# Row units moved to other weight steps, constants loaded behind the keys of head 0, and query banks summed into SBUF, in a hybrid attention layer on one Trainium2 core

## The chip, the core and the metric

The kernel runs on one core of a Trainium2 chip. The core has a matrix engine (TensorE, PE in the profile), a vector engine (VectorE, DVE), a scalar engine for activations and copies (ScalarE, ACT), a general engine (GpSimd, POOL) and SyncE (SP), which here only issues transfers. Each engine works through a queue of its own in order. They meet through semaphores. Data lies in SBUF (128 partitions), matmuls write to PSUM (8 banks of 128 x 512 floats), inputs come from HBM by DMA.

The metric is the device time of one execution in microseconds (us). The kernel before took 1256.5 us, the median of 3 runs from 1255.31 to 1256.72.

## What is computed

One layer with 256 latent tokens `x` and 256 context tokens `ctx`, 2048 wide, in float32. The context passes through the same weights and only feeds keys and values.

```python
h   = layer_norm(x)   * (1 + scale)   + shift      # scale, shift from silu(c) @ w_mod
h_c = layer_norm(ctx) * (1 + scale_c) + shift_c
aq, ak, av, az, bq, bk, bv, bz, bg, mga, mgb = split(h @ w_in)     # the same for h_c
y_a = neighbourhood_attention(aq, ak, av, ak_c, av_c, bias)        # 16 heads of 64
y_b = gated_linear_attention(rope(bq), rope(bk), bv, gates(bg), context parts)  # 4 heads
p_a = (y_a * silu(az)) @ w_br_a
p_b = (rms(y_b) * silu(bz)) @ w_br_b
out = (sigmoid(mga) * p_a + sigmoid(mgb) * p_b) @ w_out
x_new = layer_norm(2 ** 0.25 * x + gate * out)
```

## The kernel before

**Precision.** Matmuls run in a rounded float format. Each operand is therefore split into a rounded part and the rest: `split` casts on ACT (`hi`, line 148) and subtracts on DVE (`lo`, line 150). Three matmuls (hi x hi, hi x lo, lo x hi) stand for one product.

**Weights.** `load` (line 155) fetches one unit of weights, 128 x 1024 floats (704 columns for `av`), by SP into a `raw` tile, and splits it into `h_` and `l_` tiles. There are 4 `raw` buffers and 3 each of `hi` and `lo`. The loads are counted; `events` holds work that is hung on a load's number. The matmuls of a unit follow. The loads of the part that matters here: 1 to 4 are the queries `aq` of attention pairs 0 and 1, 5 to 12 the values `av` of group 0; 13 to 24 and 25 to 36 are the same for pairs 2, 3 and 4, 5; 37 and 38 are `aq6`, 39 and 40 the keys `ak7`, 41 and 42 `aq7`; 43 to 46 are the keys of head 0 of the gated linear attention (`keys(0)`), 47 to 50 its queries, 51 to 58 keys and queries of head 1, and so on.

**Row units.** `attended` needs the normalised tokens with tokens in rows, split, in chunks of 128 columns. `rows_of_h` (line 410) makes them, in 8 units of two chunks. A unit has three steps. `fetch_and_scale` issues two DMAs on SP behind the DMA of its load, `xr` (the tokens) and `sb` (the modulation, from a scratch tensor in HBM); both go to `raw` tiles; then eight DVE instructions (lines 425 and 426) scale and shift. `parts` splits the result into `rh` and `rl`, which release the `xr` tile. `store` writes both to `hrows` in HBM by two DMAs on SP. Before, unit n fetches at load 6 + 6n, splits at 7 + 6n and stores at 11 + 6n, so the last one at loads 48, 49 and 53. `rh` and `rl` come from `staging` (line 407), two buffers in all, which the constants `cs` (rope tables) and `wg` (gate weights) use as well.

**Constants.** Lines 635 to 644, behind the set-up of the last attention pair and ahead of `keys(0)`: four DMAs on POOL's queue (`cs`, `wr`, `bgt`, `ngt`) and the split of `wr` into `wg`. `gates` reads `wg` for the last time in head 3, `rope_of` reads `cs` for the last time there too.

**Query banks.** `project_x` (line 374) multiplies the latent tokens with a unit pair. It leaves two halves of a PSUM bank, 256 columns each, whose sum is the result. ACT copies the upper half to SBUF (`low`), DVE adds it to the lower half in the bank. The callers read the bank then: `project_pair` (line 475) makes `qh` and `ql` with four ACT and four DVE instructions on 64 partitions each (lines 493 to 500), `queries` (line 693) scales it on ACT, and `gated_a` (line 848) takes a sigmoid and a product of it. The banks of the pairs, `acc`, are four; `value_columns` (line 576) needs all four for its tiles `va`.

**Order.** The program is written in one order, and a planner orders each engine's queue from it ahead of time: an instruction that comes earlier in the program goes first among those that its model thinks ready. `issue_after` pins some behind others. A tile of a tag with few buffers takes one that the planner thinks free. [...]

**Head 0 to `attended`.** After the attention pairs come `keys(0)`, `turn_gates`, `gates(0)`, `queries(0)` and `decayed(0)`, and then heads 1 and 2. `attended(0)` (line 793) takes heads 0 and 1 through 16 passes: `gather` fetches a chunk of `hrows` to a `raw` tile (`hr`) and multiplies it with the weights of attention (12 matmuls, `g`), `project` loads a unit of `wv` and multiplies (12 matmuls, `o`). Between passes 7 and 9 it starts head 2's scores, `gates(3)`, and keys, queries and `decayed(3)` of head 3. `attended(1)` does heads 2 and 3.

Of the kernel before, what the change touches and what calls it, by code (L numbers as in the profile page):

```python
# [8 lines left out]
F32 = mybir.dt.float32  # L9
F32R = mybir.dt.float32r  # L10
U8 = mybir.dt.uint8
AF = mybir.ActivationFunctionType
ALU = mybir.AluOpType
# [3 lines left out]
P = 128  # L17
D = 2048
KT = 16
T = 256  # L20
# [4 lines left out]
NH = 4  # L25
# [3 lines left out]
NEG = -1.0e30  # L29
NC = 4  # L30
HELD = 4
SHARES = (
    ((0, 512, False), (512, 512, True), (1024, 512, False), (1536, 512, False)),
    ((0, 512, False), (512, 256, True), (1024, 512, False), (768, 256, True), (1536, 256, False), (1792, 256, False)),
# [54 lines left out]
def tile_backbone_layer(  # L89
# [21 lines left out]
    nc = tc.nc  # L111
    const = ctx.enter_context(tc.tile_pool(name="const", bufs=1))
# [12 lines left out]
    def k4(shape, name, dt=F32):  # L125
        return work.tile(shape, dt, tag="k4", name=name, bufs=4)

    def k2(shape, name, dt=F32):
        return work.tile(shape, dt, tag="k2", name=name, bufs=5)
# [13 lines left out]
    def mm(o, a, b, start, stop):  # L143
        return nc.tensor.matmul(o, a, b, start=start, stop=stop).ins  # L144
# [8 lines left out]
    loads, events = [], {}  # L153
# [12 lines left out]
    def unit(name, k):  # L166
        return load(wst[UNIT_AT[name, k]], 1024, f"{name}_{k}")
# [203 lines left out]
                mm(dst, wl[:, c], hhi[:, 0:2, a, :], False, False)  # L371
                mm(dst, wh[:, c], hlo[:, 0:2, a, :], False, a == KT - 1)

    def project_x(name, dst):
        for k in range(0, KT, 8):
            wh, wl = unit(name, k)
            for i in range(8):
                a = k + i
                c = slice(P * i, P * i + P)
                if a:  # L380
                    mm(dst[:, :T], wl[:, c], hhi[:, 0, a, :], False, False)
                mm(dst, wh[:, c], hl[:, :, 0, a, :], a == 0, a == KT - 1)
                if a == 0:
                    mm(dst[:, :T], wl[:, c], hhi[:, 0, a, :], False, False)
        low = k2([P, T], f"low_{name}")
        nc.scalar.copy(low[:], dst[:, T:])
        nc.vector.tensor_tensor(out=dst[:, :T], in0=dst[:, :T], in1=low[:], op=ALU.add)

    def project_rows(dst, wh, wl, k, w, tiles):
        for t in range(tiles):  # L390
# [16 lines left out]
    def staging(shape, name, dt=F32R):  # L407
        return const.tile(shape, dt, tag="staging", name=name, bufs=2)
# [31 lines left out]
        return fetch_and_scale, parts, store  # L440

    for n in range(8):
        events.setdefault(6 + 6 * n, []).append(lambda dma, sub, n=n: rows_event(n, dma, sub))

    def rows_event(n, dma, sub):
        fetch, parts, store = rows_of_h(n)
        fetch(dma, sub)
        events.setdefault(7 + 6 * n, []).insert(0, parts)
        events.setdefault(11 + 6 * n, []).insert(0, store)

    store_modulation()

# [12 lines left out]
    for p in range(K0):  # L465
        dst = kTs[p // 4][:, p % 4, :]
# [8 lines left out]
    def project_pair(p, q):  # L475
        kT = kTs[p // 4][:, p % 4, :]
        if p >= K0:
            kp = acc(f"kp{p}")
            project_t(f"ak{p}", kp[:])
            nc.scalar.copy(kT, kp[:])  # L480
        kn = k2([P, 512], f"kn{p}", F32R)
        kl = k2([P, 512], f"kl{p}", F32R)
        split(kn[:], kl[:], kT, loads[-2] if p >= 2 else None)
        kh = k4([P, 2, 512], f"kh{p}", F32R)
        for j in range(2):
            for r, src in zip(half, (kn, kl)):
                nc.gpsimd.dma_start(kh[r, j, :], src[half[j], :])
        qp = acc(f"qp{p}")
        project_x(f"aq{p}", qp[:])
        qh, ql = q[:, p % 2, 0], q[:, p % 2, 1]  # L490
        for j in range(2):
            r, o = half[j], half[1 - j]
            nc.scalar.mul(qh[r, j, :], qp[r, :T], 0.125)
            nc.vector.scalar_tensor_tensor(
                ql[r, j, :], qp[r, :T], 0.125, qh[r, j, :].bitcast(F32), ALU.mult, ALU.subtract
            )
            nc.scalar.mul(qh[o, j, :], qp[r, :T], 0.125)
            nc.vector.scalar_tensor_tensor(  # L498
                ql[o, j, :], qp[r, :T], 0.125, qh[r, j, :].bitcast(F32), ALU.mult, ALU.subtract
            )  # L500
        return qh, ql, kh

    def attention(p, qh, ql, kh):
# [70 lines left out]
    low = []  # L574
# [19 lines left out]
    def turn_gates():  # L594
        lp = bank("lp")
        for t in range(4):
            nc.tensor.transpose(lp[:, P * t : P * t + P], low[0][:, t].rearrange("p r c -> p (r c)"), ident[:])
        nc.scalar.copy(lr[:], lp[:])
        for r in (slice(32, 64), slice(96, 128)):
            nc.vector.tensor_tensor(out=lr[r, :], in0=lp[r, :], in1=lr[r, :].bitcast(F32), op=ALU.subtract)  # L600

    probs = {}
    for g in range(3):
# [4 lines left out]
        n = len(loads) + 1  # L608
# [13 lines left out]
    n = len(loads)  # L622
# [9 lines left out]
    at(n + 14, (read_values, 7))  # L632


    cs = staging([P, 3, T], "cs", F32)
    wg = staging([P, 2, 512], "wg")
    wr = k4([P, 2, 512], "wr")
    bgt = const.tile([P, NH, 2], F32, name="bgt")
    ngt = const.tile([P, 4], F32, name="ngt")
    for t, src in ((cs, rope), (wr, wg2), (bgt, bg2), (ngt, ng)):  # L640
        nc.gpsimd.dma_start(t[:], src)
    nc.scalar.copy(wg[:], wr[:])
    lo = slice(64, 128)
    nc.vector.tensor_tensor(out=wg[lo], in0=wr[lo], in1=wg[lo].bitcast(F32), op=ALU.subtract)
    def rope_of(dst, src, name, eng):
        t = k2([P, 2, T], f"rt_{name}")
        for a in range(2):
# [6 lines left out]
    def gates(h):  # L654
        zp = pair(f"z{h}")
        for d in range(2):
            mm(zp[:, d, :], wg[:, d, P * h : P * h + P], lr[:], True, True)
        ga = k4([P, 2, 512], f"ga{h}")
        gm = k4([P, 2, 512], f"gm{h}")
        for d in range(2):  # L660
            b = bgt[:, h, d : d + 1]
            nc.scalar.activation(ga[:, d, :], zp[:, d, :], AF.Abs, bias=b)
            nc.vector.tensor_scalar(gm[:, d, :], zp[:, d, :], b, 0.0, ALU.add, ALU.min)
        nc.scalar.activation(ga[:], ga[:], AF.Exp, scale=-1.0)
        nc.scalar.activation(ga[:], ga[:], AF.Ln, bias=1.0)
        nc.vector.tensor_tensor(out=gm[:], in0=gm[:], in1=ga[:], op=ALU.subtract)

        cum = k2([P, 2, T], f"cum{h}")
        dec = k2([P, 2, T], f"dec{h}")

        def scan(o, i):
            nc.vector.tensor_tensor_scan(o, i, i, 0.0, ALU.add, ALU.bypass)

        scan(cum[:, 0, :], gm[:, 0, :T])
        scan(cum[:, 1, :][:, ::-1], gm[:, 1, :T][:, ::-1])
        nc.vector.memset(dec[:, 0, T - 1 : T], 0.0)
        nc.vector.memset(dec[:, 1, 0:1], 0.0)
        scan(dec[:, 0, : T - 1][:, ::-1], gm[:, 0, T + 1 :][:, ::-1])
        scan(dec[:, 1, 1:], gm[:, 1, T : 2 * T - 1])
        nc.scalar.activation(dec[:], dec[:], AF.Exp, scale=1.0 / 16.0)  # L680
        return cum, dec

    def keys(h, own=None):
        kf = k4([P, 2, 512], f"kf{h}")
        for a in range(2):
            bp = acc(f"bk{h}{a}")[:] if own is None else own[:, a, :]
            project_t(f"bk{h}{a}", bp)
            nc.scalar.copy(kf[:, a, :], bp)  # L688
            if hooks:
                hooks.pop(0)()  # L690
        return kf

    def queries(h, room=acc):
        qf = k2([P, 2, T], f"qf{h}")
        for a in range(2):
            bp = room(f"bq{h}{a}")
            project_x(f"bq{h}{a}", bp[:])
            nc.scalar.mul(qf[:, a, :], bp[:, :T], 1.0 / 16.0)
        return qf

    def decayed(h, cum, dec, kf, qf):
# [145 lines left out]

    def gated_a(p, room=acc):
        zp = room(f"az{p}")
        project_x(f"az{p}", zp[:])  # L850
        sg = k2([P, T], f"sga{p}")
        nc.scalar.activation(sg[:], zp[:, :T], AF.Sigmoid)
        nc.vector.tensor_tensor(out=sg[:], in0=sg[:], in1=zp[:, :T], op=ALU.mult)
        nc.vector.tensor_tensor(out=ya[:, p, :], in0=sg[:], in1=ya[:, p, :], op=ALU.mult)

    pws = [weights_of(0)]
    kf = keys(0)
    turn_gates()
    decays = gates(0)
    kq = kf, queries(0)  # L860
    parts = decayed(0, *decays, *kq)
    decays = gates(1)
    kq = keys(1), queries(1)
    parts1 = decayed(1, *decays, *kq)
    hooks.append(lambda: scores(0, parts, pws[0]))
    kf = keys(2)
    decays = gates(2)
    kq = kf, queries(2)
# [151 lines left out]
    fin, gb, zs, zt0 = tail[:, 0:4], tail[:, 4], (tail[:, 5], tail[:, 6]), tail[:, 7]  # L1020
# [3 lines left out]
    for g in range(4):  # L1024
        bp = bank(f"gb{g}")
# [53 lines left out]
    for u in range(8):  # L1079
        src = wst[UNIT_AT[f"wo{NC - 1}", 2 * u]]  # L1080
        if u < HELD:
            raw = stream.tile([P, 1024], F32, tag="raw", name=f"r_last{u}", bufs=4)
# [3 lines left out]
            split(wh, wl, raw[:])  # L1086
        elif u == HELD:
            raw = stream.tile([P, 1024], F32, tag="raw", name=f"r_last{u}", bufs=4)
# [38 lines left out]
    op = acc("wol_0")  # L1127
    last_mm(op[:], 0, 0, 512)
    residual(op[:], 0, NC - 1, base, base + 512, nc.vector)
    finish(0, *statistics(0, NC), SHARES[0])  # L1130
    for i in range(2):
        op = acc(f"wol_1{i}")
# [9 lines left out]
    r, q = tiny([P, 1], "rr"), tiny([P, 1], "rt")  # L1142
# [109 lines left out]
```

## Time and profile before

| what | value |
|---|---|
| median of 3 runs | 1256.5 us |
| the profiled execution's own time | 1255.54 us |
| its span, from the first to the last instruction | 1253.8 us |
| granted TensorE clock, mean | 0.99 |
| read from HBM, written to it | 247.66 MB, 10.52 MB |
| hardware DMA queue of SP (q1) | 59.3% of 16 engines' span |

The profile comes from one execution. A page shows each engine's busy time as a share of the span, and groups of instructions by line. `out<-in` names the tile that is written and those that are read; `xN` is the number of instructions. In the list of waits, `A <- B` says that engine A's instruction stood idle until B was done. A busy matrix engine means that a matmul was in flight. Matmuls overlap, so the distance of their starts is shorter than one takes by itself.

### The profile page before, as it was taken

Reading aid. Unit: us, or ns where it says so; the run is one execution under the profiler, and the core shown is the slowest. Engines: PE = TensorE matmul, PEld = TensorE weight load, DVE = VectorE, ACT = ScalarE, POOL = GpSimd, SP = SyncE. Lnnn points to the kernel's source line nnn. Section 1 sums busy time; section 2 is a strip of 40 time slices with the busy share of each in tenths; the row PEclk is TensorE's granted clock in tenths of the full one; section 3 lists DMA queues with packets and bytes.
Section 4 is the critical chain, followed back from the end, with each engine's and each line's share of the span. In section 5 each row is a group of like instructions: output and inputs, shape, how many; then the busy total and the mean of one; then the engine's idle time right before and its main releaser. Section 6 shows DMA issues by size and latency. Waiting matters only on the chain.

```text
span 1253.8 us, 16294 instructions
## 1 busy us (share of the span) xinstructions
PE 1211.8 (97%) x6233; PEld 996.4 (79%) x6233; DVE 773.4 (62%) x1154; ACT 545.2 (43%) x776; POOL 64.2 (5%) x87
## 2 busy tenths in 40 slices
PE   6999999999999999899899999999999999999997
PEld 5666798989878887678688888888888888888885
DVE  6655577667667565434553366676566665665677
ACT  4322455545455353533353274454444444445350
POOL 1000100000101210001000000000000000000111
PEclk9999999999999999999899999999999999999999
DMA  9997557666623333443745557777776777756661
GB/s 378 418 405 278 149 171 217 198 185 229 190 94 118 118 135 101 155 165 101 252 158 194 190 199 264 237 224 242 240 242 231 246 236 235 237 186 257 243 220 67
DMA packets 77054, 263.45 MB, mean 210 GB/s; under 512 B 8920, under 2 KB 8936, under 8 KB 71856
## 3 DMA queue, kind: packets, MB, share of 16 engines
q1 hardware_dynamic: 73616, 256.69, 59.3%
q0 software_dynamic: 2928, 5.16, 1.8%
q8 instruction: 49, 0.80, 0.3%
q10 hardware_dynamic: 432, 0.56, 0.1%
q14 instruction: 29, 0.24, 0.1%
HBM read 247.66 MB, written 10.52 MB: 206 GB/s over the span
## 4 chain that ended last, share of the span: by engine, by line
PE 79%; DVE 8%; DMA 7%; ACT 3%; issue 2%; POOL 0%; SPq 0%; DVEq 0%; ACTq 0%; POOLq 0%
PE bz L144 7%; PE mgb L144 7%; PE va L144 7%; PE pb L144 7%; PE mga L144 7%; PE kp L144 7%; PE bk L144 7%; PE g L144 5%; PE o L144 5%; PE pa L144 3%; PE wo L144 3%; DMA r_wv<-in_wst 3%; PE az L144 3%; PE bq L144 2%; PE qp L144 2%; PE gp L144 2%
## 5 line engine op out<-in xcount | busy, mean ns | idle before, releaser
L144 PE MATMUL va<-h_av,hl 128*128 128x352 f32 x384 | 97.7, 330 | 6.1 <-DVE q L498 6.1
L144 PE MATMUL kp<-hl,h_ak 128*128 128x512 f32 x256 | 87.1, 408 | 2.2 <-ACT hl L305 2.2
L144 PE MATMUL g<-ah,hr 128*128 128x512 f32 x256 | 82.4, 403 | 3.9 <-DMA hr<-hrows 3.2
L144 PE MATMUL o<-h_wv,gt 128*128 128x512 f32 x256 | 85.1, 395 | 0.2 <-ACT h_wv L148 0.2
L144 PE MATMUL bk<-hl,h_bk 128*128 128x512 f32 x256 | 80.8, 392 | 0.7 <-ACT kf L688 0.7
L144 PE MATMUL bz<-h_bz,hl 128*128 128x512 f32 x256 | 80.6, 392 | 0.0
L150 DVE TENSOR_TENSOR l_wv<-r_wv,h_wv 128x1024 fp32r<-128x1024 f32 x32 | 39.1, 1224 | 67.0 <-ACT h_wv L148 66.9
L144 PE MATMUL mgb<-h_mgb,hl 128*128 128x512 f32 x256 | 79.7, 390 | 0.0
L144 PE MATMUL mga<-h_mga,hl 128*128 128x512 f32 x256 | 79.4, 389 | 0.0
L144 PE MATMUL pb<-h_pb,hl 128*128 128x512 f32 x256 | 79.4, 389 | 0.0
L144 PEld LDWEIGHTS va<-h_av,hl 128*128 128x128 f32 x384 | 68.4, 191 | 8.0 <-DVE q L498 4.3
L150 DVE TENSOR_TENSOR l_pb<-r_pb,h_pb 128x1024 fp32r<-128x1024 f32 x32 | 39.2, 1225 | 39.9 <-ACT h_pb L148 39.9
L144 PEld LDWEIGHTS kp<-hl,h_ak 128*128 128x128 f32 x256 | 48.1, 190 | 19.3 <-issue 5.3
L144 PE MATMUL va<-l_av,hl 128*128 128x352 f32 x192 | 62.5, 325 | 0.0
L144 PEld LDWEIGHTS g<-ah,hr 128*128 128x128 f32 x256 | 48.9, 193 | 16.2 <-DMA hr<-hrows 5.2
L148 ACT CAST h_wv<-r_wv 128x1024 fp32r<-128x1024 f32 x32 | 33.5, 1049 | 56.0 <-DMA r_wv<-in_wst 56.0
L150 DVE TENSOR_TENSOR l_mgb<-r_mgb,h_mgb 128x1024 fp32r<-128x1024 f32 x32 | 39.2, 1225 | 30.1 <-ACT h_mgb L148 29.9
L144 PEld LDWEIGHTS bk<-hl,h_bk 128*128 128x128 f32 x256 | 48.1, 188 | 11.3 <-ACT kf L688 1.1
L144 PEld LDWEIGHTS o<-h_wv,gt 128*128 128x128 f32 x256 | 48.1, 189 | 11.0 <-ACT h_wv L148 1.4
L150 DVE TENSOR_TENSOR l_mga<-r_mga,h_mga 128x1024 fp32r<-128x1024 f32 x32 | 39.2, 1224 | 27.5 <-ACT h_mga L148 27.5
L144 PEld LDWEIGHTS mga<-h_mga,hl 128*128 128x128 f32 x256 | 48.1, 188 | 9.9
L144 PEld LDWEIGHTS pb<-h_pb,hl 128*128 128x128 f32 x256 | 48.1, 188 | 9.9
(335 smaller groups left out, 2975.4 us busy)
## 6 DMA issues: line engine op xcount, KB each, us to landing
wm<-in_wmod SPq DMA_DIRECT2D x32, 1024.0 KB, 9.1
hr<-hrows SPq DMA_DIRECT2D x32, 512.0 KB, 3.7
r_wv<-in_wst SPq DMA_DIRECT2D x32, 512.0 KB, 3.6
r_bz<-in_wst SPq DMA_DIRECT2D x32, 512.0 KB, 3.6
wg<-in_wgate SPq DMA_DIRECT2D x64, 256.0 KB, 3.7
r_mga<-in_wst SPq DMA_DIRECT2D x32, 512.0 KB, 3.6
r_mgb<-in_wst SPq DMA_DIRECT2D x32, 512.0 KB, 3.4
r_pb<-in_wst SPq DMA_DIRECT2D x32, 512.0 KB, 3.3
```

The costliest lines, as they stand in the source:

```text
L144: return nc.tensor.matmul(o, a, b, start=start, stop=stop).ins
L148: cast = nc.scalar.copy(hi, src)
L150: sub = nc.vector.tensor_tensor(out=lo, in0=src, in1=hi.bitcast(F32), op=ALU.subtract)
```

## The change

It has four parts. First, the row units hang on loads 6, 11, 17, 22, 28, 32, 36 and 41, split one load later and store four loads later (before: five loads after the fetch), so the last store hangs on load 45, the third load of `keys(0)`. Second, the constants are fetched and split behind `keys(0)`. Third, `queries(0)` stands ahead of `gates(0)`. Fourth, `project_x` no longer writes back to the bank: ACT copies the upper half, scaled, into an SBUF tile `both`, DVE adds the scaled lower half to it there, and the callers read `both`. `queries` does the same into its own `qf` tile.

```diff
+ROW_STEPS = (6, 11, 17, 22, 28, 32, 36, 41)
...
-    def project_x(name, dst):
+    def project_parts(name, dst):
...
-        low = k2([P, T], f"low_{name}")
-        nc.scalar.copy(low[:], dst[:, T:])
-        nc.vector.tensor_tensor(out=dst[:, :T], in0=dst[:, :T], in1=low[:], op=ALU.add)
+
+    def project_x(name, dst, scale=1.0):
+        project_parts(name, dst)
+        both = k2([P, T], f"both_{name}")
+        nc.scalar.mul(both[:], dst[:, T:], scale)
+        nc.vector.scalar_tensor_tensor(both[:], dst[:, :T], scale, both[:], ALU.mult, ALU.add)
+        return both
...
-        events.setdefault(6 + 6 * n, []).append(lambda dma, sub, n=n: rows_event(n, dma, sub))
+        events.setdefault(ROW_STEPS[n], []).append(lambda dma, sub, n=n: rows_event(n, dma, sub))
...
-        events.setdefault(7 + 6 * n, []).insert(0, parts)
-        events.setdefault(11 + 6 * n, []).insert(0, store)
+        events.setdefault(ROW_STEPS[n] + 1, []).insert(0, parts)
+        events.setdefault(ROW_STEPS[n] + 4, []).insert(0, store)
...
-        project_x(f"aq{p}", qp[:])
+        qs = project_x(f"aq{p}", qp[:], 0.125)
         qh, ql = q[:, p % 2, 0], q[:, p % 2, 1]
         for j in range(2):
             r, o = half[j], half[1 - j]
-            nc.scalar.mul(qh[r, j, :], qp[r, :T], 0.125)
-            nc.vector.scalar_tensor_tensor(
-                ql[r, j, :], qp[r, :T], 0.125, qh[r, j, :].bitcast(F32), ALU.mult, ALU.subtract
-            )
-            nc.scalar.mul(qh[o, j, :], qp[r, :T], 0.125)
-            nc.vector.scalar_tensor_tensor(
-                ql[o, j, :], qp[r, :T], 0.125, qh[r, j, :].bitcast(F32), ALU.mult, ALU.subtract
-            )
+            for d in (r, o):
+                nc.scalar.copy(qh[d, j, :], qs[r, :])
+                nc.vector.tensor_tensor(
+                    out=ql[d, j, :], in0=qs[r, :], in1=qh[r, j, :].bitcast(F32), op=ALU.subtract
+                )
...
-            project_x(f"bq{h}{a}", bp[:])
-            nc.scalar.mul(qf[:, a, :], bp[:, :T], 1.0 / 16.0)
+            project_parts(f"bq{h}{a}", bp[:])
+            nc.scalar.mul(qf[:, a, :], bp[:, T:], 1.0 / 16.0)
+            nc.vector.scalar_tensor_tensor(qf[:, a, :], bp[:, :T], 1.0 / 16.0, qf[:, a, :], ALU.mult, ALU.add)
...
-        project_x(f"az{p}", zp[:])
+        zs = project_x(f"az{p}", zp[:])
         sg = k2([P, T], f"sga{p}")
-        nc.scalar.activation(sg[:], zp[:, :T], AF.Sigmoid)
-        nc.vector.tensor_tensor(out=sg[:], in0=sg[:], in1=zp[:, :T], op=ALU.mult)
+        nc.scalar.activation(sg[:], zs[:], AF.Sigmoid)
+        nc.vector.tensor_tensor(out=sg[:], in0=sg[:], in1=zs[:], op=ALU.mult)
...
     pws = [weights_of(0)]
     kf = keys(0)
+    cs = staging([P, 3, T], "cs", F32)
+    wg = staging([P, 2, 512], "wg")
+    wr = k4([P, 2, 512], "wr")
+    bgt = const.tile([P, NH, 2], F32, name="bgt")
+    ngt = const.tile([P, 4], F32, name="ngt")
+    for t, src in ((cs, rope), (wr, wg2), (bgt, bg2), (ngt, ng)):
+        nc.gpsimd.dma_start(t[:], src)
+    nc.scalar.copy(wg[:], wr[:])
+    lo = slice(64, 128)
+    nc.vector.tensor_tensor(out=wg[lo], in0=wr[lo], in1=wg[lo].bitcast(F32), op=ALU.subtract)
     turn_gates()
+    qf = queries(0)
     decays = gates(0)
-    kq = kf, queries(0)
+    kq = kf, qf
     parts = decayed(0, *decays, *kq)
```

The ten lines of the constants are removed from lines 635 to 644, unchanged.

More of the change, by code (lines that the diff above doesn't have):

```diff
@@ L632, in tile_backbone_layer @@
     at(n + 14, (read_values, 7))
[L635 to L644, printed above, removed]
     def rope_of(dst, src, name, eng):
```

## The prediction

> **What bounds the kernel now.** I read the page first: its first part says that TensorE (PE) is busy nearly all the time.
>
> ```profile
> span 1253.8 us, 16294 instructions
> PE 1211.8 (97%) x6233; PEld 996.4 (79%) x6233; DVE 773.4 (62%) x1154; ACT 545.2 (43%) x776; POOL 64.2 (5%) x87
> ```
>
> PE is idle for 1253.8 - 1211.8 = 42 us in all, so no edit of this kind can give more than that and what a slow clock costs. The view by stretches says where the idle time lies (columns: stretch, its length, busy time of each engine with its instructions, granted clock, DMA share, GB/s).
>
> ```profile
> 141.00:335.00 194.00, 187.94 (x1140) 171.13 (x1139) 135.32 (x225) 98.99 (x186) 16.60 (x33) 0.98 0.65 200
> 335.00:404.00 69.00, 65.96 (x329) 52.75 (x329) 50.48 (x96) 36.15 (x60) 7.01 (x5) 1.00 0.35 118
> 482.00:602.00 120.00, 109.13 (x483) 86.38 (x481) 52.99 (x86) 43.34 (x59) 4.16 (x6) 0.98 0.44 148
> 602.00:735.00 133.00, 132.41 (x600) 109.97 (x600) 54.39 (x75) 52.30 (x78) 2.87 (x3) 0.98 0.58 195
> ```
>
> 141 to 335 holds the pairs of attention heads and the values, 335 to 404 head 0 of the gated linear attention, 482 to 602 the first half of `attended(0)` with the keys of head 3 pushed into it, 602 to 735 its end and `attended(1)`. PE lacks 6, 3 and 11 us in the first three and 0.6 in the last. The waits of PE, over 141 to 480 and then over 480 to 760, name what ended them (total us, times, longest).
>
> ```profile
> PE va L144 <- DVE q L498: 6.1, 3, 2.5
> PE az L144 <- DVE l_az L150: 2.5, 1, 2.5
> PE bq L144 <- DVE l_bq L150: 1.2, 1, 1.2
> PE z L144 <- ACT pr L526: 0.8, 1, 0.8
> PE bq L144 <- ACT h_bq L148: 0.6, 1, 0.6
> PE z L144 <- DVE lr L600: 0.3, 1, 0.3
> ...
> PE ap L144 <- DVE near L743: 3.6, 1, 3.6
> PE g L144 <- DMA hr<-hrows: 3.2, 4, 1.2
> PE o L144 <- DVE l_wv L150: 1.5, 1, 1.5
> PE ap L144 <- DVE near L744: 0.8, 1, 0.8
> ...
> PE bk L144 <- DVE l_bk L150: 0.6, 1, 0.6
> ```
>
> An idle gap costs more than itself here. Behind four of these waits the same view by stretches shows half a clock:
>
> ```profile
> 156.80:160.20 3.40, 3.19 (x10) 2.94 (x11) 3.31 (x10) 1.80 (x4) 0.00 (x0) 0.51 0.00 0
> 214.80:218.20 3.40, 3.40 (x11) 3.11 (x12) 1.24 (x2) 0.78 (x1) 0.00 (x0) 0.50 0.88 279
> 518.60:522.00 3.40, 3.40 (x10) 2.64 (x9) 1.20 (x4) 1.37 (x2) 0.00 (x0) 0.50 0.43 154
> 600.50:607.30 6.80, 6.04 (x17) 4.60 (x17) 2.48 (x9) 0.00 (x0) 0.52 (x1) 0.50 0.90 314
> ```
>
> 3.4 us at half clock lose 1.7 us, the last row 3.4. The first two follow waits for `q`, the third the wait for `l_wv`, the last the wait for `near`.
>
> **Query banks: project_x into SBUF.** Now the two halves of a bank are added inside PSUM, and then four ACT and four DVE instructions read that bank one after the other; a bank is shared by no two engines at once. The bank goes to a `va` tile of the values only when the last of them is done. The chain around the first wait, from the timeline of DVE and PE:
>
> ```profile
> 155.92 0.48 DVE L425 SCALAR_TENSOR_TENSOR xr<-xr,mvs,sb 128x256 f32<-128x256 f32 x1 [3.03 <-DMA sb<-mods]
> 156.44 0.43 DVE L498 SCALAR_TENSOR_TENSOR q<-qp,q 64x256 fp32r<-64x256 f32 x1
> 157.01 0.63 PE L144 MATMUL va<-h_av,hl 128*128 128x352 f32 x1 [2.47 <-DVE q L498]
> ...
> 217.98 7.78 PE va L144 x48
> ```
>
> DVE sat 3.03 us in its queue for the rows' `sb`, the last `q` of the first pair stood behind it, and PE behind that. (The last row is from the chain that ended last: 48 matmuls in 7.78 us, 0.16 each.) After the change a bank is free after two instructions: one ACT copy and one DVE add. The work does not shrink: five instructions stay five on each engine. The new copies and subtractions out of SBUF are not in the trace in their form. The nearest rows bound them:
>
> ```profile
> L497 ACT ACTIVATE q<-qp x16: 375/379/382, 150.7 to 340.2; 64x256 fp32r<-64x256 f32 x16
> L148 ACT CAST kn<-kT 128x512 fp32r<-128x512 f32 x7 | 4.3, 619 | 0.0
> L648 DVE TENSOR_TENSOR qr<-qf,cs x8: 409/422/426, 383.0 to 592.5; 128x256 f32<-128x256 f32 x8
> ```
>
> An ACT copy takes 0.38 (nearest in size, taken) to 0.62, so at most 4 x 0.24 = 1 us more ACT per pair, and a DVE subtraction about 0.42, which is what it takes now. ACT has 95 us free in 141 to 335, so neither is on the path; without that cover the 8 pairs would cost up to 8 us. `both` holds one of five `k2` buffers some 3 us longer than `low` did (eight instructions of 0.38 to 0.43), and the next pair's `kn` and `kl` need two: I take 0 for it. The queries of the heads lose one ACT instruction per bank, also beside the path; `gated_a` keeps its count.
>
> What the path gains: the second and third waits (6.1 - 2.5 = 3.6 us) go, since two instructions of 0.4 us free a bank where ten did; with them one half-clock stretch, 1.7. At the first wait the row unit keeps its step (6), so DVE again waits for `sb`, and the add for the *second* pair can stand behind it and end near 156.9. PE then only gets on by the six matmuls of the tile that has the first bank: 6 x 0.16 = 1.0, and the gap shrinks to 1.5, at the edge of the slow clock; I leave the stretch in. **Term 1: 3.6 + 1.7 + 1.0 = 6.3 us**, between 1 (only the first effect) and 6.1 + 3.4 = 9.5.
>
> **Row units by load 45, constants behind keys(0).** Eight row units go through two `staging` tiles, and so do `cs` and `wg`. The tile views show that the units did not run when their steps say:
>
> ```profile
> L148 ACT CAST rh<-xr x8: 1044/1049/1051, 161.6 to 594.9; 128x1024 fp32r<-128x1024 f32 x8
> L150 DVE TENSOR_TENSOR rl<-xr,rh x8: 1217/1226/1226, 164.8 to 598.2; 128x1024 fp32r<-128x1024 f32 x8
> L435 SPq DMA_DIRECT2D hrows<-rl x8: 360/462/473, 170.5 to 599.5; - x8
> L419 SPq DMA_DIRECT2D xr<-in_xrow x8: 328/345/346, 146.5 to 348.5; - x8
> ```
>
> The last `xr` was fetched at 348.5 and split only at 594.9, just after the last reader of `cs` had begun (592.5, in the `qr` row above). The `parts` of units 6 and 7 come at loads 43 and 49, behind the constants in program order, so those held both staging tiles until head 3 was through, and two fetched `xr` kept two of the four `raw` buffers from about 350 to 595. In the new order the `parts` of unit 7 come at load 42, ahead of the constants, and all buffers are free by about 350. What that cost is seen in `attended(0)` against `attended(1)`, in the chain that ended last:
>
> ```profile
> 530.62 1.24 DVE l_wv L150
> 531.88 4.01 DMA r_wv<-in_wst
> 537.00 1.24 DVE l_wv L150
> ...
> 728.84 5.44 PE o L144 x24
> ```
>
> With two buffers `l_wv` frees the buffer, the next `r_wv` is fetched into it and is split: 537.00 - 530.62 = 6.4 us a pass. A pass is 24 such matmuls, 5.44 us by the last row, and with four buffers PE does it without a gap (602 to 735 above). So the waits on `hr` (3.2), `l_wv` (1.5, with 1.7 of half clock) and `l_bk` (0.6) go: 7.0. The wait for `near` (3.6 + 0.8 + 3.4 of half clock = 7.8) has two of the late units' `rl` (1.23 each) in its DVE queue, and it stands there only because the rows for the last four passes were not stored yet; with them stored, PE has passes to do meanwhile. I count 6 of the 7.8, since the order is the planner's. **Term 2: 13 us**, between 7 and 14.8.
>
> The queues: a unit issues four DMAs on SP as before, only closer (loads 28, 32, 36, 41), and four DMAs for the constants go behind the `kh` copies on POOL, which has 5% work. `wg`'s cast now stands in ACT's queue behind unit 7's store, with the splits of `bq` behind it. The bounds are 0 and the 7.4 that `cs` waits for such a store on POOL now:
>
> ```profile
> POOL cs L641 <- DMA hrows<-rl: 7.4, 1, 7.4
> ```
>
> I take 0.5, since the store leaves with load 45 and PE then has two loads of keys, 5.44 us each, and the queries ahead of `gates(0)`.
>
> **gates(0) behind queries(0).** The four waits of `z` and `bq` (0.3 + 0.8 + 1.2 + 0.6 = 2.9) go with row unit 7 and the gate chain out of that stretch. But the chain's DVE work moves to where `decayed(0)` already fills it:
>
> ```profile
> 370.00:404.00 34.00, 31.80 (x156) 25.42 (x157) 28.82 (x63) 18.60 (x32) 7.01 (x5) 1.00 0.38 130
> L672 DVE TENSOR_TENSOR_SCAN cum<-gm 128x256 f32<-128x256 f32 x8 | 5.1, 677 | 0.1
> ```
>
> Four scans of 0.68, the subtraction L666 over 1024 columns like `rl` (1.23) and two `gm` additions over 512 (an estimate: 0.7 each) make 5.4. 28.8 + 5.4 = 34.2 of 34 us: full, and it spills. The bounds are 0 (the four loads of `keys(1)` alone, 24 matmuls each, give PE 4 x 5.44 = 22 us before it needs `decayed(0)`) and 5.4 + 1.7 x 2 = 8.8, if the splits of `bk` are late and two slow stretches follow. I take 2.4. **Term 3: 2.9 - 2.4 - 0.5 = 0.** The `az` wait (2.5) comes from head 2's rope chain, which the change leaves as it is: 0.
>
> **Sum.** 6.3 + 13 + 0 = 19.3; 1253.8 - 19.3 = 1234.5 us of span. The profiled execution took 1255.5 for its 1253.8, so 1236.2; it stood 1.0 under the median of 1256.5: **1237**.
>
> **Rivals.** *DVE fills up behind queries(0)*: the spill costs its bound, 8.8 instead of 2.4, and Term 1 stays at 3. For it: the 34.2 of 34; against it: three loads can be split ahead. 1237 + 6.4 + 3.3 = 1247. Chance 0.11.
>
> *The planner again gives the constants the staging tiles early*, so the change doesn't do what it says: Term 2 is lost, 1250. Against it: in this trace the units behind the constants in program order got their tiles last. 0.04.
>
> *Slower: DVE's queue waits for sb*, as in the 155.92 row. All eight units wait, and the new steps put more of them next to the banks' adds and the splits:
>
> ```profile
> DVE xr L425 <- DMA sb<-mods: 9.6, 4, 3.8
> ```
>
> Where PE is not covered, such a wait costs up to 3.8 + 1.7 = 5.5. Four of eight eat the gain; with five the time is 1237 + 27 = 1264. Against it: of the four waits now only one stops PE at once. 0.08.
>
> *The slow clock does not come from these gaps*: then the stretches that I took off (1.7 + 1.7 + 2.6 of 3.4) stay, 1243. The trace is against it: each stands right behind a wait. 0.05. The Trainium skill, "TensorE: Matmul & The Clock Gate", section "The HAM clock gate", gives half rate after at least one idle window of about 3.4 us. By that rule only the wait of 3.6 could slow the clock; the trace does not agree, since waits of 1.5 and 2.5 us did too.
>
> *More than forecast*: every wait quoted goes, `az` too with 1.7 for its clock: 9.5 + 14.8 + 2.9 + 4.2 = 31.4, 1225. 0.10.
>
> **How the numbers follow.** The forecast itself (1229 to 1244) has 0.62. From 1225 to 1250 lie the forecast, the clock rival, and most of the first rival and of the better case: 0.8. A measurement can tell about 0.2% (2.5 us) from no change. Faster 0.87; same 0.05, from the upper ends of the first two rivals; slower 0.08.
>
> **What would show it.** Right: no wait of `va` on `q` over 1.6 us; the last `rh` before 350; passes of 5.4 us in `attended(0)`; no slow stretch around 519 and 600. Wrong: `rh` after 500 still; a wait of `bk` or `bq` on `l_bk`, `l_bq` between 360 and 420 beyond 2.4 us in all; new waits of `va` on `l_av` behind idle DVE time ended by `sb`.

## The result and the profile after

| | before | after |
|---|---|---|
| median of the runs side by side | 1256.4 us (1255.3 to 1256.7, 4 runs) | 1223.7 us (1221.6 to 1226.5, 4 runs) |
| profiled execution | 1255.5 us | 1226.5 us |
| its span and granted clock | 1253.8 us, 0.990 | 1224.8 us, 0.998 |

The ratio of the times is 0.974, 95% interval 0.972 to 0.976: 32.7 us less by the medians, 29.0 by the two profiled executions. The profiled execution of the changed kernel is the slowest of its four. The forecast of 1237 was 13 us too high, and the range (1225 to 1250) missed the time by 1.3 us. The time is that of the rival called "more than forecast" (1225), though most of its terms are not.

The page of the changed kernel, its first part:

```profile
span 1224.8 us, 16303 instructions
PE 1200.0 (98%) x6233; PEld 991.0 (81%) x6233; DVE 772.7 (63%) x1154; ACT 542.6 (44%) x768; POOL 64.0 (5%) x87
```

PE is idle for 24.8 us where it was 42. So 17 of the 29 us are idle time; the other 12 are in PE's *busy* time, 1211.8 before and 1200.0 now, for the same 6233 matmuls. The waits of PE in the changed kernel, over 141 to 480 and, last row, over 480 to 760 (total us, times, longest):

```profile
PE s L145 <- DVE q L500: 0.9, 2, 0.8
PE va L145 <- DVE both_aq L391: 0.9, 1, 0.9
PE az L145 <- DVE l_az L151: 0.7, 1, 0.7
PE s L145 <- ACT q L499: 0.6, 1, 0.6
PE o L145 <- ACT gt L149: 0.5, 1, 0.5
...
PE bk L145 <- ACT kf L680: 0.7, 1, 0.7
```

The waits for `q` before `va`, for `near`, `hr`, `l_wv`, `l_bk`, `pr` and `l_bq` are gone, `az` is down from 2.5 to 0.7, and new are the waits of the scores `s` for `q` (1.5 us in 3) and shorter ones of `o` for `gt`. The tile view of the row units shows that they now run when their steps say:

```profile
L149 ACT CAST rh<-xr x8: 1028/1048/1050, 160.9 to 315.7; 128x1024 fp32r<-128x1024 f32 x8
L151 DVE TENSOR_TENSOR rl<-xr,rh x8: 1212/1224/1226, 163.3 to 317.9; 128x1024 fp32r<-128x1024 f32 x8
```

The last `rh` starts at 315.7, not at 594.9, and in `attended(0)` the chain that ended last is PE alone. Each pass is 2.72 + 2.72 = 5.44 us, with nothing between:

```profile
488.37 2.72 PE o L145 x12
491.09 2.72 PE g L145 x12
493.81 2.72 PE o L145 x12
```

**Stretches of the same work.** To set kernels side by side I cut each one where PE starts the same matmul: number 954 (the first of `qp`), 2090 (the first of `bk`), 2820 (the first `g` of `attended(0)`) and 3990 (the first `bz`). Between two of these every kernel here runs the same number of matmuls, so a longer stretch is a cost, as far as its length repeats. The view by stretches, cut at those places, before (columns as in the prediction):

```profile
141.20:334.50 193.30, 187.24 (x1137) 170.51 (x1136) 134.86 (x224) 98.29 (x184) 16.40 (x32) 0.98 0.65 199
334.50:481.80 147.30, 141.80 (x734) 118.31 (x733) 102.49 (x208) 73.81 (x120) 20.05 (x18) 0.99 0.34 114
481.80:751.10 269.30, 257.84 (x1172) 210.45 (x1171) 120.07 (x180) 109.33 (x157) 7.03 (x8) 0.98 0.51 173
```

And after:

```profile
141.20:330.40 189.20, 186.60 (x1138) 168.82 (x1136) 139.12 (x234) 100.30 (x186) 15.86 (x31) 0.99 0.71 219
330.40:470.60 140.20, 139.38 (x734) 117.02 (x732) 98.94 (x194) 71.05 (x112) 17.52 (x18) 1.00 0.36 122
470.60:720.90 250.30, 248.91 (x1172) 208.01 (x1171) 118.75 (x185) 107.43 (x154) 9.98 (x9) 1.00 0.51 174
```

I call them A (pairs and values; Term 1), B (heads 0 to 2 up to `attended(0)`; Term 3 and the `az` wait) and C (`attended(0)` and `attended(1)` with head 3; Term 2). A lost 4.1 us, B 7.1, C 19.0; the rest of the kernel is 643.9 before and 645.1 after.

### The profile page after: what moved, and what is told of

Read it like the earlier page. It is cut to its first block, busy times and chain, and to the rows that moved or that the text cites. A ratio compares the mean times of both kernels' runs of the same rounds, so it can differ in the third digit from the quotient of the medians.

```text
span 1224.8 us, 16303 instructions
## 1 busy us (share of the span) xinstructions
PE 1200.0 (98%) x6233; PEld 991.0 (81%) x6233; DVE 772.7 (63%) x1154; ACT 542.6 (44%) x768; POOL 64.0 (5%) x87
## 4 chain that ended last, share of the span: by engine, by line
PE 78%; DVE 8%; DMA 8%; ACT 3%; issue 2%; POOL 0%; SPq 0%; DVEq 0%; ACTq 0%; POOLq 0%
PE bz L145 7%; PE mgb L145 7%; PE pb L145 7%; PE mga L145 7%; PE o L145 7%; PE g L145 7%; PE kp L145 6%; PE bk L145 5%; PE pa L145 4%; PE bq L145 3%; PE wo L145 3%; PE az L145 3%; PE va L145 2%; DMA sb<-mods 2%; PE gp L145 2%
## 5 line engine op out<-in xcount | busy, mean ns | idle before, releaser
L151 DVE TENSOR_TENSOR l_wv<-r_wv,h_wv 128x1024 fp32r<-128x1024 f32 x32 | 39.2, 1225 | 72.9 <-ACT h_wv L149 72.8
L145 PE MATMUL g<-ah,hr 128*128 128x512 f32 x256 | 79.0, 390 | 0.0
L151 DVE TENSOR_TENSOR l_pb<-r_pb,h_pb 128x1024 fp32r<-128x1024 f32 x32 | 39.2, 1225 | 39.9 <-ACT h_pb L149 39.9
L151 DVE TENSOR_TENSOR l_mgb<-r_mgb,h_mgb 128x1024 fp32r<-128x1024 f32 x32 | 39.2, 1225 | 30.1 <-ACT h_mgb L149 29.9
L145 PEld LDWEIGHTS bz<-h_bz,hl 128*128 128x128 f32 x256 | 48.1, 188 | 9.9
```

Of the source, the lines that this page charges most:

```text
L151: sub = nc.vector.tensor_tensor(out=lo, in0=src, in1=hi.bitcast(F32), op=ALU.subtract)
```

## The experiments

Times in us. "Before" was run again beside each group of kernels: its median was 1255.6 for the first four, 1254.1 for the next four, 1255.7 for the last three. A, B and C are from each profiled execution, cut as above.

| kernel | A | B | C | median (range) | ratio to before, 95% |
|---|---|---|---|---|---|
| before | 193.3 | 147.3 | 269.3 | 1256.4 | 1 |
| after | 189.2 | 140.2 | 250.3 | 1223.7 (1221.6 to 1226.5) | 0.972 to 0.976 |
| banks only | 184.7 | 147.3 | 268.7 | 1246.7 (1246.1 to 1246.9) | 0.991 to 0.996 |
| new steps only | 193.8 | 141.8 | 251.8 | 1235.3 (1233.0 to 1237.8) | 0.981 to 0.987 |
| after, old banks | 195.2 | 140.2 | 252.6 | 1233.7 (1231.9 to 1237.4) | 0.979 to 0.987 |
| after, two buffers held | 186.5 | 140.9 | 262.7 | 1236.9 (1235.6 to 1237.3) | 0.983 to 0.988 |
| after, gates(0) first | 191.1 | 142.4 | 250.4 | 1226.4 (1224.6 to 1230.6) | 0.975 to 0.980 |
| after, old steps | 184.0 | 141.0 | 251.8 | 1223.5 (1222.5 to 1224.7) | 0.972 to 0.977 |
| after, later scores | 185.1 | 140.2 | 250.9 | 1222.5 (1221.5 to 1226.7) | 0.972 to 0.977 |
| ... and later first units | 184.7 | 140.2 | 250.7 | 1222.2 (1220.6 to 1224.7) | 0.972 to 0.976 |
| after, one buffer held | 185.1 | 140.2 | 250.5 | 1223.0 (1222.5 to 1224.4) | 0.972 to 0.976 |
| constants moved only | 191.8 | 141.9 | 253.1 | 1235.1 (1232.5 to 1238.5) | 0.981 to 0.986 |
| after, a second profile | 186.3 | 140.2 | 250.9 | 1223.4 (1221.8 to 1224.1) | 0.972 to 0.976 |

The theory after the result: three parts add up, the banks (A), the row units in time (C, through the `raw` buffers and the stored rows), and what late units did to B. The rivals: one part does all; or a part gains only together with another; or the buffers have nothing to do with it.

### The banks alone

The kernel before with the sums of the query banks taken into SBUF (`project_x`, `project_parts`, and their uses for pairs, queries and gates), and nothing else:

```diff
-        project_x(f"aq{p}", qp[:])
+        qs = project_x(f"aq{p}", qp[:], 0.125)
...
-            nc.scalar.mul(qh[r, j, :], qp[r, :T], 0.125)
...
+                nc.scalar.copy(qh[d, j, :], qs[r, :])
```

> The kernel before with the query banks summed into SBUF alone; row units, constants and gates as before. Theory (the terms add up): the waits of va on q (6.1 us and two slow stretches of 1.7) fall to about 1 us, the late row units stay: 1256.4 - 8 = 1248, between 1245 and 1251; the last rh still near 595. Rival (the wait for sb in DVE's queue is what stops PE, and the bank only shows it): va waits on both instead of q for 4 us or more, 1253 or above.

Measured: 1246.7, 8.9 less than before. All of it is in A; B and C stand as before:

```profile
140.80:325.50 184.70, 183.83 (x1137) 167.92 (x1137) 134.19 (x224) 98.58 (x184) 16.47 (x33) 1.00 0.69 209
325.50:472.80 147.30, 142.09 (x734) 118.06 (x733) 103.25 (x205) 70.93 (x113) 17.94 (x17) 0.99 0.34 114
472.80:741.50 268.70, 257.74 (x1172) 210.54 (x1171) 121.25 (x184) 109.80 (x156) 9.97 (x9) 0.98 0.51 173
```

The clock of A is 1.00 where it was 0.98: both slow stretches behind waits for `q` went, and the first wait, for which I had left 1.5 us and its slow stretch in, is 0.9 and slows nothing. B has its old length from other parts: `az` waits 1.3 us with no slow stretch behind it, and a slow one at 366.0, behind waits of `bq` and `z`, is new.

### The new steps alone

The kernel before with the row units' steps changed; the constants stay ahead of keys(0):

```diff
+ROW_STEPS = (6, 11, 17, 22, 28, 32, 36, 41)
...
-        events.setdefault(6 + 6 * n, []).append(lambda dma, sub, n=n: rows_event(n, dma, sub))
+        events.setdefault(ROW_STEPS[n], []).append(lambda dma, sub, n=n: rows_event(n, dma, sub))
```

> The kernel before with the new row steps alone; constants stay ahead of keys(0), banks as before. Theory: staging tiles go out in the program order of their first writers, so unit 7's parts at load 42 come ahead of the constants and this alone frees the raw buffers: rh ends before 350, passes of 5.4 us in attended(0), 1256.4 - 17 = 1239, between 1235 and 1243. Rival (the constants must stand behind keys(0), or the planner gives them the tiles early): rh after 500 as before, 1252 or above.

Measured: 1235.3, 20.3 less. It is in B (5.5) and C (17.5), and A is no shorter (193.8 to 193.3). My Term 2 had 13 for this edit together with the constants' place.

### The whole change without the banks

The changed kernel with `project_x` and its uses as before:

```diff
-        qs = project_x(f"aq{p}", qp[:], 0.125)
+        project_x(f"aq{p}", qp[:])
...
-        zs = project_x(f"az{p}", zp[:])
+        project_x(f"az{p}", zp[:])
```

> The changed kernel with the query banks added in PSUM again, as before. Theory: the waits of va on q come back, 1223.7 + 8 = 1232, between 1229 and 1236. Rival (new steps alone took the units away from the banks, so the banks' edit is worth little): 1224 to 1227.

Measured: 1233.7, 10.0 over the changed kernel, and 6.0 of the profiled 8.4 are in A (195.2 to 189.2); 2.3 are in C, where `g` waits 1.9 us for `sga`, the tile that `gated_a` makes of its bank. The parts add up: 8.9 (banks) + 20.3 (steps) = 29.2 of 32.7, and the rest is the order of gates(0) (1.6 in B: 141.8 to 140.2 between these two kernels) and scatter of a few us.

### Two raw buffers held

The changed kernel, in which two of the four `raw` buffers belong to idle tiles from keys(0) to the end of decayed(3) (328.7 to 586.3). The rows are split and stored in time, so this has the buffers of the kernel before without its late rows.

```diff
     turn_gates()
+    holds = [stream.tile([P, 1024], F32, tag="raw", name=f"hold{i}", bufs=4) for i in range(2)]
+    for t in holds:
+        nc.gpsimd.memset(t[:, :8], 0.0)
     qf = queries(0)
```

> The changed kernel in which two raw buffers are held by idle tiles from the keys of head 0 until decayed(3), as the two late xr tiles held them before; rows are stored early as in the changed kernel. Theory (buffers): passes of about 6.4 us in attended(0) and waits of g on hr again, 1223.7 + 9, between 1229 and 1237. Rival (what cost time were the late stores of the last rows and the order that they forced): passes of 5.4 us, 1224 to 1226.

Measured: 1236.9, 13.2 over the changed kernel, and C is 262.7, 12.4 longer. The chain that ended last now goes round through load, split and load:

```profile
516.55 1.24 DVE l_wv L151
...
517.81 4.32 DMA r_wv<-in_wst
...
522.15 1.06 ACT h_wv L149
...
523.23 1.24 DVE l_wv L151
```

523.23 - 516.55 = 6.7 us a pass against 5.44. There is no wait for `near`. The waits of PE from 468 to 605 make 6.7 us without the last row, which stands in every kernel:

```profile
PE g L145 <- DMA hr<-hrows: 2.5, 3, 1.2
PE o L145 <- ACT h_wv L149: 1.4, 4, 0.7
PE o L145 <- DVE l_wv L151: 1.2, 1, 1.2
PE bk L145 <- ACT h_bk L149: 0.8, 1, 0.8
PE bk L145 <- DVE l_bk L151: 0.8, 1, 0.8
PE bk L145 <- ACT kf L680: 0.7, 1, 0.7
```

How can 6.7 us of waits cost 12.4? The stretch C of this kernel:

```profile
468.70:731.40 262.70, 254.83 (x1171) 206.84 (x1170) 118.56 (x182) 107.68 (x154) 10.64 (x11) 1.00 0.50 169
```

Idle are 262.7 - 254.8 = 7.9 us, 6.5 more than in the changed kernel (250.3 - 248.9 = 1.4). The other 5.9 us are busy time (254.83 to 248.91), at a granted clock of 1.00 and for the same matmuls. The timeline of PE shows where they sit:

```profile
501.60 0.39 PE L145 MATMUL g<-al,hr 128*128 128x512 f32 x1
502.73 1.20 PE L145 MATMUL o<-h_wv,gt 128*128 128x512 f32 x4 [0.74 <-ACT h_wv L149]
505.12 0.50 PE L145 MATMUL o<-l_wv,gt 128*128 128x512 f32 x1 [1.18 <-DVE l_wv L151]
505.45 0.39 PE L145 MATMUL o<-h_wv,gt 128*128 128x512 f32 x1
505.69 0.40 PE L145 MATMUL o<-l_wv,gt 128*128 128x512 f32 x1
505.92 0.39 PE L145 MATMUL o<-h_wv,gt 128*128 128x512 f32 x1
...
510.72 0.50 PE L145 MATMUL o<-l_wv,gt 128*128 128x512 f32 x1
511.06 0.40 PE L145 MATMUL o<-h_wv,gt 128*128 128x512 f32 x1
```

In a running row the next matmul starts 0.23 us after the last (505.69 to 505.92), though each shows as 0.39 long, because they overlap. Ahead of a pause the last one runs out alone: 0.39 - 0.23 = 0.16 of what shows as busy is lost. Behind the pause the first takes 0.33 to the next start (505.12 to 505.45), 0.10 more. So a pause costs its idle time and about 0.26 us besides (my estimate from these rows). Between the matmuls of C the trace has 19 gaps here and 3 in the changed kernel; 16 x 0.26 = 4.2 us of the 5.9. The rest fits steps that are stretched without any gap, as the one of 0.34 from 510.72 to 511.06: its `l_wv` was done only just ahead.

### gates(0) ahead of queries(0)

```diff
-    qf = queries(0)
     decays = gates(0)
-    kq = kf, qf
+    kq = kf, queries(0)
```

> The changed kernel with gates(0) ahead of queries(0) again; the constants stay behind keys(0). Theory (Term 3 is small: the four waits of z and bq went with row unit 7, not with the order): 1225 us, between 1222 and 1229; z waits of under 1.5 us in all come back around 350, and DVE's busy time between 370 and 404 changes by less than 6 us. Rival (the order was a gain that the prediction missed): 1231 or more, with over 2.9 us of waits of z, bq and bk between 335 and 404. Second rival (the order costs, as the prediction took it): below 1222.

Measured: 1226.4, as the theory had it; the place of the waits was missed, since no wait of `z` came back. B is 142.4 against 140.2, through a wait of `bk` on `l_bk` (0.8) and one of `tp` (0.6), so the order gains about 2 us (1.6 in the pair of kernels above):

```profile
332.50:474.90 142.40, 140.11 (x732) 117.09 (x731) 98.75 (x194) 71.09 (x112) 17.31 (x19) 1.00 0.37 124
```

### The old steps in the changed kernel

```diff
-ROW_STEPS = (6, 11, 17, 22, 28, 32, 36, 41)
+ROW_STEPS = (6, 12, 18, 24, 30, 36, 42, 48)
...
-        events.setdefault(ROW_STEPS[n] + 4, []).insert(0, store)
+        events.setdefault(ROW_STEPS[n] + 5, []).insert(0, store)
```

> The changed kernel with the old row steps (6, 12, 18, 24, 30, 36, 42, 48, store five loads behind). Theory (what counts is that a unit behind the constants keeps a raw buffer and its rows come late): units 0 to 6 split before 400, unit 7 alone after 450; waits of l_wv, h_wv, hr or near come back in attended(0), 3 to 10 us in all; 1231 us, between 1226 and 1238. Rival (the units' place among the pairs of heads is what gained): with no unit late the time is over 1231 and the new waits are va, s, z or bq waits before 404; or, if the closer steps gained nothing at all, 1222 to 1225.

Measured: 1223.5, the time of the changed kernel. I had expected 1231. The rows came as the theory said (unit 6 at 316.4, unit 7 at 527.1), but one late unit costs next to nothing:

```profile
L149 ACT CAST rh<-xr x8: 1047/1051/1055, 160.3 to 527.1; 128x1024 fp32r<-128x1024 f32 x8
```

```profile
141.20:325.20 184.00, 183.77 (x1138) 167.91 (x1136) 135.37 (x225) 99.74 (x184) 15.30 (x30) 1.00 0.69 209
...
466.20:718.00 251.80, 249.60 (x1172) 207.90 (x1171) 119.94 (x183) 108.70 (x155) 9.98 (x9) 1.00 0.52 179
```

C is 1.5 longer than after, A 5.2 shorter (2.3 against the second profile of the changed kernel, below): PE is idle for 0.2 us in all of A, and the `s` waits are gone. With the constants behind keys(0), the new steps give about 1 us in C, and what they cost in A is not clear of A's scatter (below); the medians are the same.

### The constants' place alone

The kernel before with one block moved; old steps, old banks, gates(0) first:

```diff
-    cs = staging([P, 3, T], "cs", F32)
-    wg = staging([P, 2, 512], "wg")
...
     kf = keys(0)
+    cs = staging([P, 3, T], "cs", F32)
+    wg = staging([P, 2, 512], "wg")
...
```

> The kernel before with one edit, the constants behind keys(0); old row steps, old banks, gates(0) ahead of queries(0). Theory (the place of the constants behind unit 6 decides: only unit 7 is then late): unit 6 split before 350, unit 7 after 450; from the first matmul of g on the time falls by 16 to 18 us, to 749 to 751, and before it by 0 to 6; 1233 us, between 1229 and 1238. Rival (the new steps are needed as well): unit 6 late again or waits for near and l_wv as before, 1245 to 1256.

Measured: 1235.1, 20.6 less than before: as much as the new steps alone. Unit 7 alone is late (unit 6 was cast at 324.5):

```profile
L148 ACT CAST rh<-xr x8: 1045/1049/1055, 160.8 to 536.2; 128x1024 fp32r<-128x1024 f32 x8
```

```profile
475.20:728.30 253.10, 249.58 (x1171) 207.90 (x1170) 119.51 (x183) 109.90 (x157) 8.53 (x9) 1.00 0.52 178
```

So two edits do the same thing, and either is enough: the gain comes when no more than one unit stands behind the constants.

### One raw buffer held

As with two, with `range(1)`.

> The changed kernel with one raw buffer, in place of two, held by an idle tile from keys(0) to the end of decayed(3). Theory (three buffers are enough for a pass of two loads in 5.44 us, two are not): 1225 us, between 1222 and 1228, passes in attended(0) of 5.4 to 5.6 us, waits of o, g and bk on splits and rows there under 2 us more than in the changed kernel. Rival (each held buffer costs its share of the 13 us that two cost): 1230 us, between 1228 and 1233.

Measured: 1223.0, and C is 250.5 against 250.3:

```profile
466.80:717.30 250.50, 249.23 (x1172) 208.00 (x1171) 119.00 (x182) 107.82 (x154) 10.33 (x10) 1.00 0.51 176
```

One buffer of four costs nothing, two cost 12.4 us: a threshold, not a price per buffer.

### Later scores, later units

The new wait of `s` and the half clock behind it looked like 3 us to be had.

```diff
-    at(n + 2, (s0, 0))
+    at(n + 3, (s0, 0))
```

> The changed kernel with the first scores of pair 6 one load later. Theory (the s waits of 1.55 us and the half clock of 1.7 us behind them come from q copies that stand behind a split whose load came late): both go, 3.2 us less, 1220.5 us, between 1219 and 1223; no half clock between 300 and 320. Rival (the wait only moves, since the load of r_aq takes 8.8 us there whatever PE does): 1222 to 1225, with a wait of qp or va of over 1 us between 300 and 320.

Measured: 1222.5 (1221.5 to 1226.7), where I had expected 1220.5. The `s` waits and the slow stretch went, and A is 185.1, but the median lies within the scatter of the changed kernel. With the first two row units later besides:

```diff
-ROW_STEPS = (6, 11, 17, 22, 28, 32, 36, 41)
+ROW_STEPS = (8, 12, 17, 22, 28, 32, 36, 41)
```

> As the kernel before it, and in addition the first two row units at steps 8 and 12 in place of 6 and 11. Theory (the wait of va on both_aq of 0.9 us that is left stands behind the DVE queue's wait for sb of unit 0): it goes, 1219.6 us, between 1217 and 1222. Rival (a bank's own add is late there whatever the row unit does): the wait stays at 0.7 to 1.0, and the time is that of the kernel before it within 1 us; or the unit's sb wait stops another bank, and it is 1 to 4 us more.

Measured: 1222.2 (1220.6 to 1224.7), where I had expected 1219.6. The wait of `va` on `both_aq` went too; the time cannot be told from the one before it.

### A second profile of the changed kernel

> The changed kernel as it is, a second profile. Theory (the s waits of pair 6 belong to the kernel: its q copies stand behind a split whose load comes late): waits of s on q of 1 to 2 us in all near 310 again, half a clock behind them, 189 us from the first matmul of qp to the first of bk. Rival (they belong to that one execution, the slowest of its four, in which one load of r_aq took 8.8 us): s waits under 0.5 us, 184 to 186 us in that stretch, profiled time under 1224. Median either way 1221 to 1226.

Measured: 1223.4, and A lies between the two theories:

```profile
141.40:327.70 186.30, 184.88 (x1138) 167.64 (x1136) 139.58 (x234) 100.47 (x186) 15.22 (x30) 1.00 0.70 220
327.70:467.90 140.20, 139.43 (x734) 117.00 (x732) 98.96 (x194) 71.08 (x112) 18.09 (x19) 1.00 0.38 126
467.90:718.80 250.90, 248.90 (x1172) 207.99 (x1171) 118.71 (x185) 107.54 (x154) 9.98 (x9) 1.00 0.50 173
```

The `s` waits are there (0.8 in 2) but short, and no slow clock follows. B and C repeat within 0.6. So the 3 us between this profile and the first one are A's: the `s` waits belong to the kernel, their length and the slow clock to the execution. Up to the end of A the kernels with two buffers or one held and with gates(0) first run the same instructions in the same order: there A is 186.5, 185.1 and 191.1, the last with another wait (`qp`, 2.2 us) and a slow stretch behind it. So A scatters by 6 us from one execution to the next, and a smaller difference of A between two profiles shows nothing by itself. Against before this profile has A -7.0, B -7.1, C -18.4: 32.5 us, which is what the medians show.

## Why the prediction was wrong

The sum was 6.3 (Term 1, A) + 13 (Term 2, C) + 0 (Term 3 and `az`, B) = 19.3. The second profile has 7.0 + 18.4 + 7.1. Direction, mechanisms and most named waits were right; the sizes of Term 2 and Term 3 were not, by 5.4 and 7.1.

**Term 2, the two `raw` buffers: the first step that failed.** I put 7.0 on them, the idle time of the waits for `hr`, `l_wv` and `l_bk` with one slow stretch; holding two buffers measured 12.4. The waits view counts only PE's idle time. A loop that needs 6.4 to 6.7 us a pass where PE needs 5.44 stops PE many times for short moments, and each stop takes some 0.26 us that show as busy, so 5.9 of the 12.4 stood in no list of waits. My own row had most of the answer: (6.4 - 5.44) x 10 passes = 9.6, and 12.6 with the 6.7 measured here; I summed only the waits that the list named. The other part of Term 2 was right: for the late rows (the wait for `near`) I counted 6 of 7.8, and C of the kernel with the banks alone, which has both faults, is 268.7 - 262.7 = 6.0 longer than that with two buffers held and rows in time (a difference: no kernel had both units' rows late and all buffers free). One `staging` tile came free earlier than I had it: `rh` of unit 6 was written at 505.8, but its `rl`, which releases the `xr` tile, only at 593.6. The step "two units stand behind the constants and hold two buffers" holds: C falls to 251.8 when no unit stands there (new steps only) and to 253.1 when one does (constants moved only), and two idle tiles in their place bring 12.4 of it back.

**Term 3, taken as 0, gave 7.1: the second step that failed, and the larger miss.** Of the 7.1, 2.9 are the waits of `z` and `bq`, 1.8 the `az` wait, 1.7 the slow stretch behind it, and 0.7 other busy time. Three of its numbers were off. The waits of `z` and `bq` (2.9) went as I said, and they went with the late units: B falls from 147.3 to 141.9 and 141.8 with either edit alone, gates(0) still first. Held buffers do not explain that: alone they cost B 0.7 (140.9 to 140.2). What else the late units held up there was not separated. The spill of DVE (2.4) and the cast behind the store (0.5) did not come: the order of gates(0), which I costed as a loss, gains about 2 us. The stretch that I had filled to 34.2 of 34 us has

```profile
370.00:404.00 34.00, 33.90 (x167) 27.30 (x166) 29.88 (x64) 19.25 (x27) 4.86 (x4) 1.00 0.28 93
```

29.88 us of DVE, and PE idle for 0.1. I had added the gate chain to a stretch as if all else in it stayed. DVE has 1.1 us more there than before, not 5.4, though the work itself also stands some 4 us earlier now, so the two windows don't hold quite the same; where each piece of the chain runs I did not trace. And the `az` wait, "left as it is: 0", fell from 2.5 to 0.7, with its slow stretch of 1.7. I gave it to head 2's rope chain. In the two kernels of the table that have two buffers taken (banks only; two held) it is 1.3, in all with them free 0.6 to 0.7, so part of it was the buffers again. What made up the rest, from 2.5 to 1.3, I did not separate.

**Term 1 was right in sum, partly by luck.** The banks alone give 8.6 in A, not 6.3: the first wait shrank to 0.9, below my 1.5, and did not slow the clock. The new instructions cost what I took (copies 0.40 us, subtractions 0.42 in the changed kernel). The new steps take 1.6 (second profile) to 4.5 us (first) of it back, a size that lies within A's scatter. They do it through the scores of pair 6: with the new steps `s` waits for `q` in every kernel but the two with later scores (0.2 to 2.6 us), with the old steps in none. I put it down to unit 7's work, which stands in the queues next to the splits on which those `q` copies depend; that was not tried by itself.

**The rivals.** DVE did not fill up. The planner did not give the constants the staging tiles early. The slower rival's waits did come, as this row of DVE's waits over the whole span shows, in place of 9.6 in 4 before:

```profile
DVE xr L430 <- DMA sb<-mods: 11.3, 6, 3.4
```

but only the short new waits on `q` can be put down to them, if any; PE had other work next to the rest. That the slow clock does not come from the gaps is refuted: with the gaps, all six slow stretches behind waits went (10.2 us), and one new wait brought one back. "More than forecast" had 0.10; it was the only case that took every wait at its full price, and its time came partly by luck: its terms were right for B (2.9 + 4.2 = 7.1), while it had 9.5 for A, where 4.1 to 7.0 came, and 14.8 for C, where 18.4 to 19.0 came. It deserved more because three of my deductions (1.8 of `near`, 2.9 in Term 3, the first stretch of Term 1) were cautions without a row that showed a loss.

## What to carry to other kernels

Where a stage is limited by a loop of load, split and buffer, price it by the loop's period against PE's own period times the number of passes; the list of waits shows only a part of it. Look for what holds buffers across a stage boundary in program order: the first use decides who gets a staging tile, and two late holders of four buffers cost 12.4 us here where one cost nothing. To compare kernels, cut their traces at the same matmul: it turned a sum of guesses into lengths that repeat within 1 us in B and C. Cut so, A differed by 6 us between executions of the same instructions: a stretch needs a second profile before a small difference in it is read.

## What the runs showed of the hardware

A pause of TensorE costs more than its idle time: about 0.26 us (an estimate) of what the profile counts as busy. With matmuls stretched without a gap, this made 5.9 us in one stretch of 263.

In the changed kernel PE was idle for 3.40 - 1.85 = 1.55 us of a window, in three short gaps, and the next 3.4 us ran at half clock:

```profile
308.90:312.30 3.40, 1.85 (x6) 0.90 (x6) 3.29 (x7) 1.50 (x4) 0.00 (x0) 1.00 0.37 114
...
312.40:315.70 3.30, 3.30 (x9) 2.57 (x8) 3.30 (x9) 1.05 (x1) 0.00 (x0) 0.50 0.10 41
```

That is less idle time than the Trainium skill, "TensorE: Matmul & The Clock Gate", section "The HAM clock gate", gives for the slow clock (one idle window of about 3.4 us).

The slow stretches of one execution lie on a grid: in the kernel before they start at 156.7, 214.8, 477.6, 518.6 and 600.5, and the steps between these are 17, 77, 12 and 24 times 3.413 us, to 0.1 us. Each time the clock was full before, and the window of the grid just ahead had 1.55 us or more of idle time, in this kernel and in all the others here. But in the kernel before, a window of its grid with 3.40 - 1.76 = 1.64 us idle kept the clock:

```profile
269.40:272.80 3.40, 1.76 (x10) 1.63 (x11) 2.78 (x4) 1.34 (x3) 0.00 (x0) 1.00 0.58 175
272.80:276.20 3.40, 3.40 (x23) 3.40 (x22) 2.62 (x3) 1.19 (x2) 0.00 (x0) 1.00 0.70 191
```

So what counts here seems to be the share of idle time in a window of the grid, with a limit near 1.6 of 3.4 us, but idle time as the profile shows it does not decide alone; no run varied it by itself.
